# An encoder layer on one core: h made in token order, GpSimd's products moved, and the first expert's bias added last

## The chip, the core and the metric

One core of a Trainium2 chip runs one layer on 256 frames. The metric is the time of one execution in microseconds (us), the median of the runs.

## What is computed

The layer has a stem, a mixer of two head groups, and a mixture of experts; each ends in a LayerNorm with a residual (ALPHA is the fourth root of 2):

```
h = layer_norm(x, ln_in_g, ln_in_b)                       # x: 256 x 1024
gq, gk, gv, gg, glr, rq, rk, rv, rg = split(h @ w_in)     # 3088 columns
o_gla = rms_norm(chunk_attention(gq, gk, gv, decay(glr))) * silu(gg)
o_ret = group_norm(chunk_attention(rotary(rq), rotary(rk), rv, fixed decay)) * silu(rg)
h = layer_norm(ALPHA * h + concat(o_gla, o_ret) @ w_out)
gates = softmax(top4(h @ router_w + router_b))            # 32 experts
for each expert e of a frame:                             # 1024 -> 2048 -> 1024
    y += gate * (clamped_swiglu(h @ w1[e] + b1[e]) @ w2[e] + b2[e])
out = layer_norm(ALPHA * h + y)
```

## The kernel before

**Stages.** The stem normalises x in token order (tile `xt`), turns it by eight TensorE transposes per half of the frames, applies scale and shift per channel from the columns `cols`, and splits the result into a high part `hTh` and a low part `hTl` (`hT`, lines 211 to 248). Every large product of the mixer is made as three products (high x high, low x high, high x low), in `proj_T` (line 255: channels by frames, for gqk, rqk and the two gates) and `values` (line 352: frames by channels, for gv and rv). `split` (line 198) makes the two parts of a piece of weight: ScalarE copies the high part, VectorE (for the first two pieces of gqk GpSimd) subtracts for the low one; three buffers of high parts and two of low ones turn over. `keep_warm` puts transposes of the identity on TensorE, 18, 18 and 14 of them, in the stem.

GpSimd also makes the residual copy `res` of h (lines 333 to 336, from two broadcast loads of 512 KB of scale and shift), four of the decay products and copies in the gated group (lines 381 to 392), the rotation of rq and rk (lines 399 to 404, behind eight ScalarE copies that swap halves), four products in the second gate group (line 537), and the low parts of the biases (`bt`, lines 662 to 672).

**Experts.** The experts go in 16 pairs of up to 64 seats an expert. For a pair, `gather` (line 693) picks the rows by one-hot products into `px` and turns them into `xg`, `hidden` (line 738) puts the bias into four PSUM banks (`set_bias`) and adds the products of w1 in eight k steps, and `outputs` does the same for w2. `in_order` holds TensorE to program order here. The gate softmax is in `finish_routing` (line 674), run from `middle(0)` behind the second k step of pair 0.

**Loads.** All loads go out on SP in order. Weights of the experts, 1 MB a load, go into a ring of 20 buffers (`order`, line 842) that are the mixer's own buffers until it frees them; after the first 21 loads each next one waits until TensorE has used a buffer. The order on each engine comes from a scheduler; `issue_after` puts an instruction behind another of its engine.

Of the kernel before, what the change touches and what calls it, by code (L numbers as in the profile page):

```python
# [12 lines left out]
F32 = mybir.dt.float32  # L13
# [7 lines left out]
P = 128  # L21
# [6 lines left out]
E = 32  # L28
# [5 lines left out]
WARM = (18, 18, 14)  # L34
# [9 lines left out]
def tile_layer(ctx: ExitStack, tc: tile.TileContext, x, positions, rows_d, bc_d, gate_d, w_in, wglr_d,  # L44
# [46 lines left out]
    for t in range(NT):  # L91
        nc.sync.dma_start(xt[:, t, :], x[0, t * P:(t + 1) * P, :])
# [4 lines left out]
    gatew, glrT = gatew[0:32], glrT[0:32]  # L97
    nc.sync.dma_start(rows[:NROW], rows_d)
# [3 lines left out]
    nc.sync.dma_start(posi, positions.to_broadcast([P, S]))  # L102
# [5 lines left out]
    w_gqk = w_cols(0, "w_gqk", (0, 1))  # L108
    nc.sync.dma_start(w_glr, wglr_d.rearrange("p (k n) -> p k n", k=KC))
    nc.sync.dma_start(gatew, gate_d)  # L110
# [19 lines left out]
    G.memset(glrT, 1.0)  # L130
# [23 lines left out]
    cols = const.tile([P, NROW], F32, name="cols")  # L154
    pc = bank("m", "pc")
    pc_done = T.transpose(pc[:, :NROW], rows[:NROW], ident[:NROW, :NROW])
    cols_done = A.activation(cols, pc[:, :NROW], AF.Copy)
    keep_warm(WARM[1], pc_done)
# [15 lines left out]
    def rstd_act(var, name):  # L174
# [5 lines left out]
        newton(y, w, None, vh)  # L180
        return y
# [14 lines left out]
    highs = []  # L196

    def split(src, k, n, name, into=None, eng=V):
# [5 lines left out]
        with tc.issue_after(first_h.ins) if len(highs) == 2 else ExitStack():  # L204
            highs.append(A.activation(hi, src, AF.Copy))
        eng.tensor_sub(lo, src, hi.bitcast(F32))
# [4 lines left out]
    hTh, hTl, hT = (slot(i, nm, dt).rearrange("p (q t k s) -> p q t k s", q=2, t=NT, k=4)  # L211
                    for i, nm, dt in ((11, "hTh", F32R), (12, "hTl", F32R), (14, "hT", F32)))
    pts = {}
    for t in range(NT):
# [4 lines left out]
        with tc.issue_after(cols_done.ins) if t else ExitStack():  # L219
            r = rstd_act(mv[:, 1:2], f"ln0_{t}")  # L220
        V.tensor_scalar(xt[:, t, :], xt[:, t, :], mv[:, 0:1], r, op0=ALU.subtract, op1=ALU.mult)
    preload(TRIG, rstd_exp[-1])
    for t in range(NT):
        for q in range(2):
            pts[t, q] = bank("h", f"phT{t}{q}").rearrange("p (k t) -> p k t", k=4)
            for k in range(4):
                c = 4 * q + k
                last_tr = T.transpose(pts[t, q][:, k, :], xt[:, t, c * P:(c + 1) * P], ident)
    keep_warm(WARM[2], last_tr)
    for q in range(2):  # L230
        for t in range(NT):
            for k in range(4):
                c = 4 * q + k
                gs, bs = cols[:, GIN + c:GIN + c + 1], cols[:, BIN + c:BIN + c + 1]
                if (q, t) == (0, 1):
                    A.activation(hT[:, q, t, k, :], pts[t, q][:, k, :], AF.Identity, bias=bs, scale=gs)
                else:
                    with tc.issue_after((second if t else lead).ins) if q else ExitStack():
                        V.tensor_scalar(hT[:, q, t, k, :], pts[t, q][:, k, :], gs, bs, op0=ALU.mult, op1=ALU.add)
            if (q, t) == (0, 0):  # L240
                lead = V.tensor_copy(hTh[:, q, t], hT[:, q, t])
            else:
                last_h = A.activation(hTh[:, q, t], hT[:, q, t], AF.Copy)
                if q == 0:
                    first_h = last_h
            last_l = (V if t or q else G).tensor_sub(hTl[:, q, t], hT[:, q, t], hTh[:, q, t].bitcast(F32))
            if (q, t) == (0, 1):
                second = last_l
# [6 lines left out]
    def proj_T(w, name, early=False):  # L255
# [12 lines left out]
        return ps, mm  # L268

    (pq, pk_), gqk_mm = proj_T(w_gqk, "gqk", early=True)  # L270
# [3 lines left out]
    s10 = slot(10, "ln_in")  # L274
    bg, bb = cut(s10, (D, D), (None, None))
    for v, i in ((bg, 0), (bb, 1)):
        nc.sync.dma_start(v, bc_d[i:i + 1, :].to_broadcast([P, D]))
# [8 lines left out]
    for j, pr in enumerate(proj_T(w_rqk, "rqk")[0]):  # L286
        A.activation(raw1 if j else raw0, pr, AF.Copy, scale=0.125 if j else 1.0)
# [8 lines left out]
    with tc.issue_after(last_l.ins):  # L296
# [20 lines left out]
    ghi, glo = split(w_glr, KC, 16, "glr")  # L317
    for i, (a, b) in enumerate(((ghi, hTh), (glo, hTh), (ghi, hTl))):
        for k in range(KC):
            T.matmul(pglr[0:16, 0:S].rearrange("p (t s) -> p t s", t=NT), a[:, k, :], chunk(b, k), start=(k == 0 and i == 0), stop=(k == KC - 1 and i == 2))  # L320
    V.tensor_copy(glrT[0:16, :], pglr[0:16, 0:S])
# [9 lines left out]


    res = const.tile([P, NT, D], F32, name="res")
    for t in range(NT):
        G.tensor_mul(res[:, t, :], xt[:, t, :], bg)
        G.tensor_add(res[:, t, :], res[:, t, :], bb)
# [15 lines left out]
    def values(w, v, name):  # L352
        pv = [bank("h", f"p_{name}{t}") for t in range(NT)]
        for k in range(KC):
            hi, lo = split(w[k // 4][:, k % 4:k % 4 + 1, :], 1, 512, f"{name}{k}")
            for t in range(NT):
# [7 lines left out]
    values(w_gv, gv, "gv")  # L364
# [7 lines left out]
    V.tensor_copy(ends, b4[:, :, CH - 1:CH])  # L372
# [702 lines left out]
```

## Time and profile before

| | before |
|---|---|
| median of 3 runs | 1105.64 us |
| lowest and highest run | 1101.23 and 1106.08 us |
| the profiled execution, its own time | 1102.8 us |
| its span, first to last instruction | 1101.0 us |
| matmul busy on TensorE (PE) | 1013.8 us (92%) |
| VectorE (DVE) busy | 284.2 us (26%) |
| ScalarE (ACT) busy | 170.4 us (15%) |
| GpSimd (POOL) busy | 70.8 us (6%) |
| loads on the SP queue | 423.81 MB, 94.5% of the 16 DMA engines' span |

A busy share is an average over the whole span; the mixer fills the first 160 us, the experts the rest. PE's ends are modelled, so a busy PE is not PE at its peak. Idle time is put down to what ended last before it.

### The profile page before, as it was taken

The numbers are of one execution on the slowest core, as the hardware profiler recorded it, in microseconds if no ns is written. First come the engines' busy times: TensorE is split into PE (matmuls) and PEld (weight loads), VectorE is DVE, ScalarE is ACT, GpSimd is POOL, SyncE is SP. The second block draws the span as 40 slices with busy tenths as digits, with TensorE's granted clock in tenths as the row PEclk, the third lists the DMA queues.
The fourth block names the chain that finished last, engine by engine and source line by source line (L and its number), as shares of the span: only waits on it lengthen the run. The fifth ranks groups of instructions, "written<-read, shape, count | busy, mean of one in ns | idle before, by whom it ended". The sixth has DMA issues, their size and how long they took to land. (4 is left out here: it accounts for less than half of the span.)

```text
span 1101.0 us, 12046 instructions
## 1 busy us (share of the span) xinstructions
PE 1013.8 (92%) x4896; PEld 462.2 (42%) x4896; DVE 284.2 (26%) x572; ACT 170.4 (15%) x347; POOL 70.8 (6%) x115
## 2 busy tenths in 40 slices
PE   7889989999999999999999999898989898999974
PEld 7768863333333343243424243333333342434322
DVE  7666951120202030321112020212010120202014
ACT  4465531101010101010101010101001010111010
POOL 5130320000000000000000000000000000000001
PEclk9889999999999999899999999999999999989997
DMA  9835869999999999999999999999999999999993
GB/s 333 327 115 197 332 232 383 420 419 419 420 419 419 420 420 419 420 420 419 420 421 418 419 421 419 418 421 419 418 420 421 419 419 421 419 419 421 419 375 128
DMA packets 70574, 424.65 MB, mean 386 GB/s; under 512 B 7187, under 2 KB 11758, under 8 KB 22382
## 3 DMA queue, kind: packets, MB, share of 16 engines
q1 hardware_dynamic: 70512, 423.81, 94.5%
q8 instruction: 40, 0.66, 0.2%
q14 instruction: 22, 0.18, 0.0%
HBM read 422.74 MB, written 1.05 MB: 385 GB/s over the span
## 5 line engine op out<-in xcount | busy, mean ns | idle before, releaser
L724 PE MATMUL ph<-w,xg 128*64 128x512 f32 x2048 | 471.1, 602 | 31.8 <-DMA w<-in_moe_w_dram 31.6
L724 PEld LDWEIGHTS ph<-w,xg 128*64 128x64 f32 x2048 | 150.4, 138 | 342.9 <-issue 273.8
L724 PE MATMUL py<-w,aT 128*64 128x512 f32 x960 | 217.4, 609 | 0.0
L836 DVE TENSOR_TENSOR acc<-acc,po 128x512 f32<-128x512 f32 (+1 forms) x62 | 41.5, 670 | 392.3 <-PE po L832 392.3
L724 PEld LDWEIGHTS py<-w,aT 128*64 128x64 f32 x960 | 70.9, 140 | 137.0 <-issue 133.7
L766 DVE TENSOR_SCALAR glu<-ph 128x512 f32<-128x512 f32 x32 | 22.0, 687 | 330.6 <-PE ph L724 330.6
L767 ACT ACTIVATE ph<-glu 128x512 f32<-128x512 f32 x32 | 19.3, 602 | 534.9 <-DVE glu L766 534.9
L703 PEld LDWEIGHTS px<-hot,res 128*128 128x128 f32 x512 | 58.4, 192 | 13.0 <-DVE glu L769 11.4
L703 PE MATMUL px<-hot,res 128*128 128x128 f32 x512 | 61.6, 278 | 0.7 <-DVE hot L709 0.7
L832 PE MATMUL po<-y,gT 128*128 128x512 f32 (+1 forms) x132 | 59.8, 594 | 0.5 <-ACT y L965 0.5
L795 ACT ACTIVATE y<-py 128x512 f32<-128x512 f32 x30 | 17.9, 597 | 216.7 <-PE py L724 216.7
L735 POOL CAST bsel<-sel 128x128 fp32r<-128x128 f32 x16 | 4.6, 289 | 633.6 <-PE py L730 623.4
L832 PEld LDWEIGHTS po<-y,gT 128*128 128x128 f32 x132 | 23.6, 189 | 36.0 <-issue 34.9
L730 PE MATMUL py<-bt,bsel 64*128 64x512 f32 x30 | 14.7, 495 | 18.2 <-ACT aT L778 18.2
L716 ACT ACTIVATE xg<-px,cols 128x128 f32<-128x128 f32 x64 | 24.0, 456 | 46.5 <-PE px L703 46.5
L803 POOL TENSOR_TENSOR hog<-hot,gate 128x128 f32<-128x128 f32 x32 | 12.2, 400 | 210.8 <-PE pg L807 202.9
L768 DVE TENSOR_SCALAR ph<-ph 128x512 f32<-128x512 f32 x32 | 22.2, 694 | 2.4 <-PE ph L724 1.3
L718 DVE TENSOR_SCALAR xg<-px,cols 128x128 f32<-128x128 f32 x64 | 21.8, 402 | 2.8 <-PE px L703 2.8
L770 DVE SCALAR_TENSOR_TENSOR glu<-ph,glu 128x512 f32<-128x512 f32 x32 | 21.9, 685 | 0.6
L769 DVE TENSOR_TENSOR glu<-glu,ph 128x512 f32<-128x512 f32 x32 | 21.6, 675 | 0.0
L777 PE MATMUL pa<-ident,glu 128*128 128x128 f32 x128 | 18.3, 284 | 2.0 <-DVE glu L770 2.0
L777 PEld LDWEIGHTS pa<-ident,glu 128*128 128x128 f32 x128 | 16.6, 207 | 3.1 <-DVE glu L770 3.1
(293 smaller groups left out, 711.3 us busy)
## 6 DMA issues: line engine op xcount, KB each, us to landing
w<-in_moe_w_dram SPq DMA_DIRECT2D x376, 1024.0 KB, 19.9
w_out<-in_w_out_dram SPq DMA_DIRECT2D x4, 1024.0 KB, 6.6
w<-in_moe_w_dram SPq DMA_DIRECT2D x8, 512.0 KB, 14.8
w<-in_moe_w_dram SPq DMA_DIRECT2D x16, 256.0 KB, 6.2
w_gqk<-in_w_in_dram SPq DMA_DIRECT2D x2, 1024.0 KB, 10.0
w_rqk<-in_w_in_dram SPq DMA_DIRECT2D x2, 1024.0 KB, 11.6
w_gv<-in_w_in_dram SPq DMA_DIRECT2D x2, 1024.0 KB, 14.6
w_rv<-in_w_in_dram SPq DMA_DIRECT2D x2, 1024.0 KB, 16.2
```

The lines of the kernel that those rows point to most:

```text
L703: in_order(lambda: T.matmul(px[c // 4][:, c % 4, :], res[:, t, c * P:(c + 1) * P], hot[:, t, :], start=(t == 0 and c % 4 == 0), stop=(t == ...
L716: A.activation(xg[:, c, :], px[c // 4][:, c % 4, :], AF.Identity, bias=bs, scale=gs)
L718: V.tensor_scalar(xg[:, c, :], px[c // 4][:, c % 4, :], gs, bs, op0=ALU.mult, op1=ALU.add)
L724: in_order(lambda: T.matmul(ps[i * CAP:(i + 1) * CAP, :], lhs[:, k, i * CAP:(i + 1) * CAP], ws[i], start=False, stop=last, skip_group_chec ...
L766: V.tensor_scalar(glu, pglu, 7.0, None, op0=ALU.min)
L767: sig = A.activation(pglu, glu, AF.Sigmoid, scale=1.702)
L768: V.tensor_scalar(plin, plin, 7.0, -7.0, op0=ALU.min, op1=ALU.max)
L769: V.tensor_mul(glu, glu, pglu)
L770: V.scalar_tensor_tensor(glu, plin, 1.0, glu, op0=ALU.add, op1=ALU.mult)
L777: in_order(lambda: T.transpose(pa[:, k, :], units[:, k // 2, k % 2, :], ident))
L832: in_order(lambda: T.matmul(po[:, 0:n], gT[:, t, :], y[:, at:at + n], start=True, stop=True))
L836: V.tensor_add(acc[:, t, at:at + n], acc[:, t, at:at + n], po[:, 0:n])
```

## The change

**The stem.** The two halves of x go out on two queues. Scale and shift of the stem come as one row (`gb0`), and four one-row products spread them over all frames in PSUM. VectorE centres, scales and shifts in token order, straight into `res`, in halves of the channels (`centred`, `stem`); the transposes then read `res`, and both parts of h come from PSUM. The second half of the channels is made inside the first projection. `cols` is made there too. The warm-up transposes become 10, 8 and 6.

**The mixer.** The halves of rq and rk are swapped by eight DMAs on SP, and the load of W_out's third quarter now waits for the rotation, whose buffer it takes. The decay products go between the splits of rv as `fill`, all on VectorE, the copies on ScalarE; the rotation is all VectorE's. The gate's low rank takes 16 products of 48 and 16 columns instead of 24 of 16. Half of the gated group's scaling by the norm goes to ScalarE, and in the second gate group ScalarE scales and VectorE multiplies.

**The first expert.** The bias splits come behind the gathered rows (`load_biases`, from `middle(0)`), their low parts on VectorE; pair 0 adds its bias last; the gate softmax is issued behind `xg`.

```
-WARM = (18, 18, 14)
+WARM = (10, 8, 6)
...
-        nc.sync.dma_start(xt[:, t, :], x[0, t * P:(t + 1) * P, :])
+        (nc.scalar if t else nc.sync).dma_start(xt[:, t, :], x[0, t * P:(t + 1) * P, :])
+    gb0 = slot(10, "ln_in").rearrange("p (a n) -> p a n", a=2)
+    nc.scalar.dma_start(gb0[0:1], bc_d.rearrange("(o a) n -> o a n", o=1))
...
+            spread_ = T.matmul(spreads[a, q], ones[0:1, :], gb0[0:1, a, q * 512:(q + 1) * 512], start=True, stop=True)
...
+    def centred(t, q):
...
+            return V.scalar_tensor_tensor(res[:, t, qs], xt[:, t, qs], mvs[t][:, 0:1], spreads[0, q], op0=ALU.subtract, op1=ALU.mult)
...
+    def stem(q):
...
+                lasts["n"] = V.scalar_tensor_tensor(res[:, t, qs], res[:, t, qs], rs[t], spreads[1, q], op0=ALU.mult, op1=ALU.add)
...
+                    lasts["t"] = T.transpose(pt[:, k, :], res[:, t, c * P:(c + 1) * P], ident)
+            lasts["h"] = A.activation(hTh[:, q, t], pt, AF.Copy)
+            lasts["l"] = V.tensor_sub(hTl[:, q, t], pt, hTh[:, q, t].bitcast(F32))
...
+                if early and not kh:
+                    lasts["p"] = mm
+                    stem(1) if j == 0 else columns()
...
+        for q in range(4):
+            nc.sync.dma_start(swaps[j][32 * q:32 * q + 32], raw[32 * (q ^ 1):32 * (q ^ 1) + 32])
...
+    for k in range(KC):
+        for n, b in ((48, hTh), (16, hTl)):
+            T.matmul(pglr[0:n, 0:S].rearrange("p (t s) -> p t s", t=NT), ghl[:, k, 0:n], chunk(b, k),
...
-    for t in range(NT):
-        G.tensor_mul(res[:, t, :], xt[:, t, :], bg)
-        G.tensor_add(res[:, t, :], res[:, t, :], bb)
...
-    G.tensor_mul(qn, gqT, enb)
-    V.tensor_mul(kn, gkT, enb)
-    G.tensor_mul(ke, gkT, eb)
...
+    rv_mm, rv_done = values(w_rv, rv, "rv", (decays, own_keys, own_queries, end_keys, lambda: V.tensor_mul(ke, gkT, eb),
+                                             lambda: V.tensor_mul(qn, gqT, enb), cross))
...
-        G.tensor_mul(swp, swp, sin[:, None, :].to_broadcast([P, 2, S]))
-        G.tensor_add(rot, rot, swp)
+    for swp, rot in zip(swaps, (rotq, rotk)):
+        with tc.issue_after(lows[-1].ins):
+            V.tensor_mul(swp, swp, sin[:, None, :].to_broadcast([P, 2, S]))
+        V.tensor_add(rot, rot, swp)
...
-                    G.tensor_mul(pr_, pr_, sl[:, h, :])
+                    A.activation(pr_, pt[:, h, :], AF.Identity, bias=cols[:, RB + c:RB + c + 1], scale=cols[:, RG + c:RG + c + 1])
+                    V.tensor_mul(pr_, pr_, sl[:, h, :])
...
+            with tc.issue_after(lasts["xa"].ins):
+                A.activation(bt[:, a, :], bs, AF.Copy)
+            for r0 in (32, 96):
+                V.tensor_sub(bt[r0:r0 + 32, a, :], bs[r0:r0 + 32], bt[r0:r0 + 32, a, :].bitcast(F32))
...
+            with tc.issue_after(lasts["xv"].ins):
+                V.tensor_scalar(ex, lx[:, t, 0:E], top[:, t, 4:5], None, op0=ALU.subtract)
...
+        if bias_last:
+            for j, b in enumerate(blocks):
+                set_bias(ps[j], bsel, b, last=True)
```

How it moves instructions is seen at three places. GpSimd between the first splits and the routing, before (`gqk_l` are the low parts of w_gqk, `res` the residual copy, `gfac` and `gcross` the decay products):

```order
L206 TENSOR_TENSOR gqk_l<-w_gqk_74,gqk_h 128x512 x2
L246 TENSOR_TENSOR hTl<-hT,hTh 128x512
L335 TENSOR_TENSOR res<-xt,ln_in 128x1024 x2
L336 TENSOR_TENSOR res<-res,ln_in 128x1024 x2
L330 MEMSET gqk 64x4x64
L403 TENSOR_TENSOR logs<-logs,gcross 128x512
L404 TENSOR_TENSOR misc<-misc,logs 128x512
L403 TENSOR_TENSOR logs<-logs,gcross 128x512
L383 TENSOR_TENSOR gfac<-gqk,decays 128x512
L381 TENSOR_TENSOR gfac<-gqk,decays 128x512
L392 COPY gcross<-gfac 128x2x64
```

and now:

```order
L214 TENSOR_TENSOR gqk_l<-w_gqk_74,gqk_h 128x512 x2
L315 CAST gscore<-rscore 128x256
L356 MEMSET gqk 64x4x64
L539 TENSOR_TENSOR misc_945<-misc_945,cols 128x256
L540 TENSOR_TENSOR misc_945<-misc_945,cols 128x256
```

The large operations of GpSimd between its first splits and the router's weights are gone from its queue.

VectorE in the second value product, as it stands now (`rv_l` are the low parts of w_rv, `decays` the exponentials):

```order
L214 TENSOR_TENSOR rv_l<-w_rv_361,rv_h 128x512 x2
L415 TENSOR_TENSOR gfac<-gqk,decays 128x512
L419 TENSOR_TENSOR gfac<-gqk,decays 128x512
L214 TENSOR_TENSOR rv_l<-w_rv_361,rv_h 128x512
L423 TENSOR_TENSOR gcross<-gqk,decays 128x512
L214 TENSOR_TENSOR rv_l<-w_rv_363,rv_h 128x512
L432 TENSOR_TENSOR gfac<-gqk,decays 128x512
L214 TENSOR_TENSOR rv_l<-w_rv_363,rv_h 128x512
L433 TENSOR_TENSOR gfac<-gqk,decays 128x512
L214 TENSOR_TENSOR rv_l<-w_rv_363,rv_h 128x512
```

Each decay product stands behind one split, and the five products of 512 columns are all here.

TensorE at the first expert, before (`px` are the gathered rows, `ph` the four banks of the first expert's product):

```order
L703 MATMUL px_1613<-hot_1610,res 128x128 x4
L730 MATMUL ph_1645<-bt,bsel_1643 128x512
L730 MATMUL ph_1646<-bt,bsel_1643 128x512
L730 MATMUL ph_1647<-bt,bsel_1643 128x512
L730 MATMUL ph_1648<-bt,bsel_1643 128x512
L724 MATMUL ph_1645<-w_00_0_1653,xg_1611 64x512
```

and now:

```order
L746 MATMUL px_1550<-hot_1547,res 128x128 x4
L767 MATMUL ph_1582<-w_00_0_1586,xg_1548 64x512
L767 MATMUL ph_1582<-w_01_0_1588,xg_1548 64x512
L767 MATMUL ph_1583<-w_00_0_1586,xg_1548 64x512
L767 MATMUL ph_1583<-w_01_0_1588,xg_1548 64x512
```

The four bias products no longer stand between the gathered rows and the first product of w1.

## Rows read from the trace of the kernel before

**Rows 1.** Busy time by stretch: stretch, us, busy per engine, PEclk, DMA share, GB/s.

```profile
166.04:1065.00 898.96, 846.77 (x3858) 327.00 (x3854) 154.70 (x289) 83.17 (x174) 16.70 (x46) 0.98 1.01 418
...
161.00:167.00 6.00, 6.00 (x22) 1.82 (x20) 0.20 (x1) 0.63 (x1) 2.48 (x2) 0.72 0.05 16
...
32.00:38.15 6.15, 6.13 (x28) 6.14 (x29) 3.54 (x8) 2.72 (x6) 0.00 (x0) 0.50 1.05 381
```

**Rows 2.** Timeline of SP at the first expert: start us, us, instruction.

```profile
157.55 1.80 SPq L669 DMA_DIRECT2D bs<-in_bias_dram  x4
166.04 3.76 SPq L914 DMA_DIRECT2D w<-in_moe_w_dram  x3
```

**Rows 3.** Waits of SP from 150 to 215: us in total, times, longest.

```profile
SPq L914 <- PE ph L724: 9.2, 2, 6.7
```

**Rows 4.** Timeline of PE, first projections; in brackets the idle time before and its releaser.

```profile
15.01 0.71 PE L265 MATMUL p_gqk<-hTh,gqk_h 128*128 128x256 f32 x4 [0.34 <-ACT hTh L243]
...
25.45 0.63 PE L265 MATMUL p_gqk<-hTh,gqk_h 128*128 128x256 f32 x4
32.02 1.22 PE L265 MATMUL p_gqk<-hTh,gqk_l 128*128 128x256 f32 x4 [5.94 <-DVE gqk_l L206]
...
39.61 0.63 PE L265 MATMUL p_rqk<-hTh,rqk_l 128*128 128x256 f32 x4
40.09 0.63 PE L265 MATMUL p_rqk<-hTl,rqk_h 128*128 128x256 f32 x4
```

**Rows 5.** Timeline of POOL: residual copy of h, and a decay product.

```profile
21.24 5.34 POOL L335 TENSOR_TENSOR res<-xt,ln_in 128x1024 f32<-128x1024 f32 x2 [5.01 <-DMA ln_in<-in_bc_dram]
26.54 4.87 POOL L336 TENSOR_TENSOR res<-res,ln_in 128x1024 f32<-128x1024 f32 x2
...
69.31 1.71 POOL L381 TENSOR_TENSOR gfac<-gqk,decays 128x512 f32<-128x512 f32 x1
```

**Rows 6.** The tile w_gqk, VectorE's splits: shortest/median/longest in ns, first and last start.

```profile
L206 DVE TENSOR_TENSOR gqk_l<-w_gqk,gqk_h x6: 679/682/2823, 18.6 to 32.7; 128x512 fp32r<-128x512 f32 x6
```

**Rows 7.** Timeline of PE, second value product.

```profile
64.66 0.39 PE L358 MATMUL p_rv<-rv_h,hTh 128*128 128x512 f32 x1
64.89 0.39 PE L358 MATMUL p_rv<-rv_h,hTl 128*128 128x512 f32 x1
...
73.61 1.22 PE L358 MATMUL p_rv<-rv_l,hTh 128*128 128x512 f32 x2 [3.81 <-DVE rv_l L206]
...
84.28 0.33 PE L419 MATMUL lo<-gfac 64*64 64x64 f32 x4
```

**Rows 8.** Timeline of PE, output projection.

```profile
137.89 0.73 PE L548 MATMUL pm<-wo_l,oTh 128*128 128x512 f32 x2 [0.96 <-DVE wo_l L206]
```

**Rows 9.** Timeline of PE, bias and first expert's product.

```profile
158.91 0.50 PE L730 MATMUL ph<-bt,bsel 64*128 64x512 f32 x2 [1.29 <-POOL bt L672]
160.25 0.49 PE L730 MATMUL ph<-bt,bsel 64*128 64x512 f32 x1 [0.84 <-POOL bt L672]
160.67 8.78 PE L724 MATMUL ph<-w,xg 128*64 128x512 f32 x32
```

**Rows 10.** Timeline of VectorE there, four pieces of gathered rows.

```profile
157.47 1.36 DVE L718 TENSOR_SCALAR xg<-px,cols 128x128 f32<-128x128 f32 x4
```

**Rows 11.** Timeline of VectorE in the stem, statistics of the second half.

```profile
5.98 1.29 DVE L217 BATCH_NORM_STATS2 ln_st<-xt 128x6 f32<-128x512 f32 x2
```

**Rows 12.** Lines 821 and 884: one-row spread, and VectorE's pass that reads it (ns).

```profile
L821 PE MATMUL h<-gb,ones x8: 587/718/1214, 441.4 to 447.3; 1*128 1x512 f32 x8
...
L884 DVE SCALAR_TENSOR_TENSOR h<-res,h x4: 676/678/686, 442.6 to 446.8; 128x512 f32<-128x512 f32 x4
```

**Rows 13.** Timeline of PE in the stem: warm-up and transposes.

```profile
7.60 3.79 PE L151 MATMUL warm<-ident 128*128 128x128 f32 x18
11.23 1.91 PE L228 MATMUL phT<-ident,xt 128*128 128x128 f32 x16
```

**Rows 14.** Timeline of PE, gate rank.

```profile
49.50 1.08 PE L320 MATMUL pglr<-hTh,glr_l 128*16 128x256 f32 x8
```

More of the change, by code (lines that the diff above doesn't have):

```diff
@@ L153, in tile_layer @@
     keep_warm(WARM[0])
[L154 to L158, printed above, removed]
+    spreads = {}
+    for q in range(2):
+        for a in range(2):
+            spreads[a, q] = bank("h", f"gb0{a}{q}")
+            spread_ = T.matmul(spreads[a, q], ones[0:1, :], gb0[0:1, a, q * 512:(q + 1) * 512], start=True, stop=True)
+    keep_warm(WARM[1], spread_)
     def small(name, n, tag, dt=F32):
@@ L179, in rstd_act @@
         rstd_exp.append(A.activation(y, y, AF.Exp, scale=-0.5))
-        newton(y, w, None, vh)
+        with tc.issue_after(after().ins) if after else ExitStack():
+            newton(y, w, None, vh)
         return y
@@ L226, in tile_layer @@
             for k in range(4):
                 c = 4 * q + k
[L228 to L248, printed above, removed]
@@ new lines, in stem, with columns @@
+                with tc.issue_after(lasts["p"].ins) if q else ExitStack():
+                    lasts["t"] = T.transpose(pt[:, k, :], res[:, t, c * P:(c + 1) * P], ident)
+            lasts["h"] = A.activation(hTh[:, q, t], pt, AF.Copy)
+            lasts["l"] = V.tensor_sub(hTl[:, q, t], pt, hTh[:, q, t].bitcast(F32))
+    stem(0)
+    for t in range(NT):
+        centred(t, 1)
+    first_h = lasts["h"]
+    keep_warm(WARM[2], lasts["t"])
+    cols = const.tile([P, NROW], F32, name="cols")
+    def columns():
+        pc = bank("m", "pc")
+        with tc.issue_after(lasts["p"].ins):
+            T.transpose(pc[:, :NROW], rows[:NROW], ident[:NROW, :NROW])
+        A.activation(cols, pc[:, :NROW], AF.Copy)
@@ L316, in tile_layer @@
     pglr = bank("m", "pglr")
[L317 to L321, printed above, removed]
+    ghl = hl.tile([P, 512], F32R, name="glr_hl", tag="wh", bufs=WH)[:, 0:KC * 48].rearrange("p (k n) -> p k n", k=KC)
+    A.activation(ghl, ident[:, 0:48][:, None, :].to_broadcast([P, KC, 48]), AF.Copy, scale=0.0)
+    A.activation(ghl[:, :, 0:16], w_glr, AF.Copy)
+    V.tensor_sub(ghl[:, :, 32:48], w_glr, ghl[:, :, 0:16].bitcast(F32))
+    for k in range(KC):
+        for n, b in ((48, hTh), (16, hTl)):
+            T.matmul(pglr[0:n, 0:S].rearrange("p (t s) -> p t s", t=NT), ghl[:, k, 0:n], chunk(b, k),
+                     start=(k == 0 and n == 48), stop=(k == KC - 1), skip_group_check=True)
+    V.tensor_copy(glrT[0:16], pglr[0:16, 0:S])
+    A.activation(glrT[32:48], pglr[32:48, 0:S], AF.Copy)
     lg = [math.log1p(-2.0 ** (-5.0 - h)) for h in range(4)]
@@ L392, in tile_layer @@
[L392 to L404 removed]
+    last_exp = [None]
@@ L736, in selector, with hidden @@
         return bsel
-    def hidden(xg, sel2, load, name, mid=None, early=None):
+    def hidden(xg, sel2, load, name, mid=None, early=None, bias_last=False):
         bsel = selector(sel2, name)
@@ L745, in hidden @@
         ps = [bank("h", f"ph{name}{b}") for b in blocks]
-        for j, b in enumerate(blocks):
-            set_bias(ps[j], bsel, b)
+        if not bias_last:
+            for j, b in enumerate(blocks):
+                set_bias(ps[j], bsel, b)
         for k in range(KC):
```

152 lines of the change are left out of this document (80 added, 72 removed).

## The prediction

> **What bounds the kernel now.** I read the page's slices first, then the busy times by stretch, then the issue queue of the loads, and last TensorE's order of time through the mixer. From 166 us on, the DMA engines are full (share 1.01, 418 GB/s) for 899 us, up to the tail of some 36 us [rows 1]. All of this is expert weights. So the end is the moment at which this stream starts, plus a length that the change does not touch, and any microsecond taken from the work before 166 us should come off the end, if the stream has nothing to catch up. It has not: just before, from 161 to 167 us, the DMA share is 0.05 [rows 1]. The ring of weight buffers is full then, and the next load goes out at 166.04, after a bias load at 157.55 [rows 2]; what it waited for is the first expert's product, up to 6.7 us at a time [rows 3]. That product starts at 160.67 [rows 9].
>
> So the question is when the first expert's product can start, and the mixer's stalls answer it. TensorE starts the first projection at 15.01, stands for 5.94 us before 32.02 until VectorE has split a piece of w_gqk [rows 4], and then runs at half clock (0.50, 1.2 GHz) until 38.15 [rows 1]. VectorE was late because its 0.68 us subtraction took up to 2.82 [rows 6] while GpSimd made the residual copy of h, 10.2 us in two rows [rows 5]. The same happens at 69 to 73.6: GpSimd multiplies decays [rows 5], TensorE waits 3.81 us for VectorE, then goes on slowly [rows 7]. Then comes a wait of 0.96 in the output projection [rows 8], and the bias rows: 1.29 and more on GpSimd's splits, although the gathered rows were coming from 157.47 on [rows 9, 10].
>
> **The change, part by part.**
>
> *Stem.* Before, 15.01 [rows 4]. Now the second half of x goes on another queue, and VectorE can hardly begin its statistics earlier than 5.98 [rows 11]; with 1.29 of them and three small operations I come to 7.8. Then two centring and two scaling passes, each like the one pass in the trace that reads SBUF and a spread row in PSUM, 0.68 [rows 12], so 2.7, and four one-column operations, together about 0.5: 11.0. A transpose is 0.12, sixteen in 1.91 [rows 13], so four of them, a copy taken as another 0.68, and the hops between the engines bring the first product to 12.6. Against it, the spread products stand ahead on TensorE: four of two passes each, 0.59 at best and 1.21 at worst for a pass, which overlap [rows 12], behind a row that lands at 6.5 or so, and eight warm products at 0.21 [rows 13]; that ends at 11 to 13 and may hold the transposes up by a microsecond or two. I take 13.3: a gain of 1.7. Ends: none of it (the four passes held up by GpSimd's two weight splits, 2.1 more, as the subtraction of [rows 6] was: -0.4), and 2.7.
> [...]
>
> *First projections.* Before, from 15.01 to 40.09 [rows 4] there are 30 groups of four products. At the pace of 39.61 to 40.09, 0.47 to 0.48 a group [rows 4], they take 14.1. Eight transposes of the second half of h now stand between them, 1.0 [rows 13], and one of the columns, 0.1: 15.2 against 25.08, a gain of 9.9, if VectorE keeps up without GpSimd's residual work beside it. Its list up to the end of gqk holds 14 passes of 0.68 and eight small ones of at most half that, 12.2, against TensorE's 12.4: tight, but the splits stand early in it. Ends: 5.0 (VectorE's list laid behind TensorE's waits, and the clock down once more) and 10.5.
>
> *Gate rank.* Three times eight products become sixteen; eight took 1.08, the pace 0.115 each [rows 14]: 0.9 less, ends 0.5 and 0.9.
>
> *Values.* Before, the second value product runs from 64.66 to 84.28 [rows 7], 19.62. It holds 48 products at 0.23 [rows 7] and a gate group of 0.47: 11.75. All of the decay products now stand on VectorE between the splits, copies on ScalarE, nothing on GpSimd. VectorE's list there is 14 passes of 0.68 and four narrow ones, some 11 to 12: again about TensorE's own time, with two buffers of slack. The rotation's swap goes from ScalarE to eight DMAs, off its path; they ride behind loads, but are read only after the last value split. I take 7.9, ends 4.0 (VectorE bound, TensorE standing for a microsecond or two, and its clock down behind it) and 8.2.
>
> *Output gates.* GpSimd's four products go to VectorE and its scaling to ScalarE; two engines, no row shows the pair, but the 0.96 of [rows 8] is the only wait there. I take 1.0 with 0 as the lower end: TensorE is busy otherwise from 84.28 on.
>
> *Bias.* The first product no longer waits for the bias rows, which are added last for pair 0. It can go when the first of the four pieces of 157.47 [rows 10] is there, at 158.0, not 160.67 [rows 9]: 2.7. Ends 2.0 and 3.5 (the gate softmax is off VectorE ahead of the pieces, too). The gate softmax then stands before the transposes of the gate behind two k steps, 8.8 us of products [rows 9]; VectorE's and GpSimd's work for it is nearer 6 and lies under that. The third bias load stays ahead of the next weight load on SP and now waits for VectorE's two first bias splits, some 3.5 us behind the first product with issue; the weight load behind it waited 5.4 for the product anyway [rows 2, 9]. Costed at nothing; if the splits come later, the stream does, one for one.
>
> *One-row loads.* A megabyte of spread scale and shift leaves the load queue, one load of W_out moves behind the rotation, tens of microseconds before its split is due; both at nothing.
>
> Sum: 1.7 + 9.9 + 0.9 + 7.9 + 1.0 + 2.7 = 24.1. The profiled execution took 1102.8, 2.8 under the median of its runs (1105.64). 1102.8 - 24.1 = **1078.7**. With all lower ends the gain is 11.1 (1091.7), with all upper ones 26.8 (1076.0). Runs lie from 1.6 below to 3.3 above the profiled one.
>
> **Rivals.**
> *VectorE becomes the bound* in gqk and the values, where both lists are within a microsecond of TensorE's. For it: these counts, and that a wait of a few microseconds was followed by half clock both times [rows 1, 7]. Against: the splits are spread out. A gain of 12 to 20, so some 1087.
> *The bias part does nothing,* since the third bias load holds SP ahead of the weights. For it: its place in the queue. Against: 5.4 us of cover [rows 2, 9]. The gain of 2.7 goes and up to two more: 1083.
> *The weights are not there.* The swaps and the late load of W_out hold SP, and the ring is short when the first expert starts. Each missing load of 1 MB is 2.5 us at 418 GB/s; four to ten of them give back 10 to 24: 1090 to 1103. Against: the idle 6 us of [rows 1], and slack in the queue all through the mixer.
> *Slower: the clock.* Warm products fall from 50 to 24, and TensorE stands idle until the row for the spread has landed. In the trace the first 36 transposes went at 0.21 to 0.23 and only those from 11.23 on at 0.12 [rows 13]. If the clock stays low from the first projection on, each microsecond of it costs half: 1078.7 plus half the stretch. It is slower than before only if it stays low for over 48 us, through the values; 63 us would give 1110. Against: behind a stand of 5.94 it came back after 6.15 [rows 1, 4].
> The Trainium skill (TensorE: Matmul & The Clock Gate, What's actually happening) says that "the default state is throttled, and activity releases the throttle". By that page the thinner warm-up is this rival's condition, while the products that follow without a stop release it, so the page leaves it a small chance.
>
> **How the numbers follow.** 0.5%, 5.5 us, is about what a measurement of this kernel can tell from no change. Forecast (1076 to 1083) 0.60; VectorE bound 0.22; bias part nothing 0.06; weights not there 0.06, a third of it under 1097; clock 0.03; and 0.03 for better than 1076. Faster: 0.60 + 0.22 + 0.06 + 0.03 + 0.02 = 0.93; same 0.04; slower 0.03. The range takes in all bounds and the scatter of the runs below: 1073 to 1092.
>
> **What would show it.** In the profile after: the first projection near 13.3, no wait over a microsecond in gqk and the values, a clock of 1.00 through the mixer, VectorE's subtractions at 0.68 throughout, the first expert's product near 137 (160.67 - 24.1 is 136.6), full DMA from some 142 on, and the same tail. The prediction is wrong if full DMA begins early and the end does not follow, or if a wait of TensorE for VectorE stands where GpSimd's work was.

## The result, and the profile after

The changed kernel takes 1084.45 us (median of four runs, 1083.38 to 1084.75), the kernel before 1104.12 (four runs, 1101.23 to 1106.08): a ratio of 0.9829, 95% interval 0.9805 to 0.9853. The forecast was 1078.7, with a range of 1073 to 1092. The profiled execution took 1084.73 instead of 1102.8: 18.1 us of the 24.1 that the sum had. So the time lies within the range, but above the band of 1076 to 1083 that had the largest chance.

Busy time by stretch of the kernel after, to be read beside [rows 1] (stretch, us, busy per engine, PEclk, DMA share, GB/s):

```profile
6.00:13.20 7.20, 7.15 (x9) 2.52 (x9) 7.13 (x18) 3.19 (x7) 1.72 (x2) 1.00 1.02 346
32.00:38.15 6.15, 6.15 (x54) 6.15 (x54) 3.10 (x7) 6.00 (x12) 0.31 (x1) 1.00 1.05 381
...
147.13:1047.00 899.87, 846.99 (x3854) 327.80 (x3850) 157.90 (x296) 83.75 (x175) 16.97 (x47) 0.98 1.01 418
1047.00:1082.90 35.90, 20.42 (x115) 9.59 (x115) 13.86 (x30) 4.61 (x9) 3.04 (x2) 0.83 0.50 166
```

The full stream is as long as before (899.87 and 898.96 us, 418 GB/s both), it only starts sooner, and the stretch from 32.00 to 38.15 that ran at 0.50 now holds 54 products instead of 28, at 1.00. The loss is in the first line: in these 7.2 us TensorE did nine things.

The stem of the kernel after, timeline of PE, answering to the first lines of [rows 4] and to [rows 13]:

```profile
6.05 7.19 PE L164 MATMUL gb<-ln_in,ones 1*128 1x512 f32 x8 [1.82 <-DMA ln_in<-in_bc_dram]
13.17 1.97 PE L156 MATMUL warm<-ident 128*128 128x128 f32 x8
14.93 1.91 PE L250 MATMUL phT<-ident,res 128*128 128x128 f32 x8
16.64 1.49 PE L156 MATMUL warm<-ident 128*128 128x128 f32 x6
17.77 1.20 PE L282 MATMUL p_gqk<-hTh,gqk_h 128*128 128x256 f32 x4
...
21.84 1.04 PE L250 MATMUL phT<-ident,res 128*128 128x128 f32 x8
```

Eight passes of the spread take 7.19 us, 0.9 each, and eight transposes 1.91, where eight of the same shape take 1.04 a little later (at 21.84). So, by these lengths, TensorE runs at 1.2 GHz through the whole stem. The column PEclk shows 1.00 there; in the stem the lengths of equal products have to be read, not that column. VectorE had the first half of the channels of h at 12.15, and the transposes began at 14.93. Timeline of VectorE, the statistics of the first half of the frames, and the two passes that end at 12.15:

```profile
5.88 1.28 DVE L233 BATCH_NORM_STATS2 ln_st<-xt 128x6 f32<-128x512 f32 x2 [5.88 <-DMA xt<-in_x_dram]
...
10.74 1.41 DVE L244 SCALAR_TENSOR_TENSOR res<-res,ln_y,gb 128x512 f32<-128x512 f32 x2
```

Later places of the same timeline, which answer to [rows 4], [rows 7] and [rows 9] (first projections' last group and the gate rank behind it; start of the second value product and what follows it; first expert's product):

```profile
41.95 0.63 PE L282 MATMUL p_rqk<-hTl,rqk_h 128*128 128x256 f32 x4
42.42 0.27 PE L344 MATMUL pglr<-hTh,glr_hl 128*48 128x256 f32 x1
...
57.02 0.48 PE L382 MATMUL p_rv<-rv_h,hTh 128*128 128x512 f32 x1
...
69.33 0.33 PE L455 MATMUL lo<-gfac 64*64 64x64 f32 x4
...
141.60 7.09 PE L767 MATMUL ph<-w,xg 128*64 128x512 f32 x32
```

Between 17.77 and 135 us TensorE has no wait long enough for the timeline to name one; before, the longest were 5.94, 3.81, 0.98 and 0.96. VectorE's splits, by tile, show why; the first answers to [rows 6]:

```profile
L214 DVE TENSOR_TENSOR gqk_l<-w_gqk,gqk_h x6: 681/692/693, 19.8 to 28.3; 128x512 fp32r<-128x512 f32 x6
...
L214 DVE TENSOR_TENSOR rv_l<-w_rv,rv_h x8: 682/688/693, 55.5 to 66.2; 128x512 fp32r<-128x512 f32 x8
```

None takes longer than 0.693 us; the longest was 2.82 before. And the issue queue of the loads at the first expert, beside [rows 2]:

```profile
145.31 1.73 SPq L710 DMA_DIRECT2D bs<-in_bias_dram  x4
147.13 1.91 SPq L962 DMA_DIRECT2D w<-in_moe_w_dram  x3
```

The third bias load went out 3.71 us behind the first product and the weight load behind it at 5.53; before, the weight load was 5.37 behind (166.04 and 160.67). That is 0.16 later, next to nothing, as costed.

### The profile page after: what moved, and what is told of

It reads as the page before. It is cut to its first block, busy times and chain, and to the rows that moved or that the text cites. A ratio compares the mean times of both kernels' runs of the same rounds, so it can differ in the third digit from the quotient of the medians.

```text
span 1082.9 us, 11976 instructions
## 1 busy us (share of the span) xinstructions
PE 1009.8 (93%) x4870; PEld 457.6 (42%) x4870; DVE 273.1 (25%) x574; ACT 168.9 (16%) x350; POOL 36.1 (3%) x90
## 5 line engine op out<-in xcount | busy, mean ns | idle before, releaser
L883 DVE TENSOR_TENSOR acc<-acc,po 128x512 f32<-128x512 f32 (+1 forms) x62 | 41.6, 671 | 391.5 <-PE po L879 391.4
L879 PEld LDWEIGHTS po<-y,gT 128*128 128x128 f32 x132 | 23.6, 189 | 36.0 <-issue 34.9
L759 ACT ACTIVATE xg<-px,cols 128x128 f32<-128x128 f32 x64 | 24.1, 458 | 44.6 <-PE px L746 44.6
```

The source lines that it names most:

```text
L759: lasts["xa"] = A.activation(xg[:, c, :], px[c // 4][:, c % 4, :], AF.Identity, bias=bs, scale=gs)
L879: in_order(lambda: T.matmul(po[:, 0:n], gT[:, t, :], y[:, at:at + n], start=True, stop=True))
L883: V.tensor_add(acc[:, t, at:at + n], acc[:, t, at:at + n], po[:, 0:n])
```

## The experiments

Four questions: what holds the stem (seven runs), what the products on GpSimd cost (four runs), what the bias order alone is worth (one run). And in all of them: does the end follow the first expert's product? Each run has one profile. Beside these runs the kernel before took 1102.75 to 1103.71 (medians), against 1104.12 beside the changed kernel, and four runs of one kernel lie 0.5 to 4.3 us apart; so times a microsecond or two apart tell little, and the readings rest on the profiles.

### The stem

**No warm-up between spread and transposes.**

```diff
-WARM = (10, 8, 6)
+WARM = (10, 0, 6)
```

> The eight warm-up products between the spread and the transposes are taken out (WARM 10, 0, 6). Theory: TensorE's own list sets the first projection. In the changed kernel VectorE has the first half of h at 12.15 us and the transposes begin at 14.93, behind a spread of 7.19 and eight warm products of 1.76; so without them the transposes begin at 13.2, the first projection near 16.1 instead of 17.77, and the end comes 1.7 earlier, 1082.7. Rival, the clock: those eight are what makes the clock rise before 18.8; without them the first projection starts 1.7 earlier but runs at the pace of half clock (0.23 a product) for about as much longer, and the end stays at 1084.4.

Timeline of PE in the stem, and the first expert's product:

```profile
13.19 1.97 PE L250 MATMUL phT<-ident,res 128*128 128x128 f32 x8
...
16.09 0.92 PE L282 MATMUL p_gqk<-hTh,gqk_h 128*128 128x256 f32 x4
...
139.20 7.09 PE L767 MATMUL ph<-w,xg 128*64 128x512 f32 x32
```

1082.03 us (1081.89 to 1085.6). The first projection starts at 16.09, 1.68 sooner. By the last transposes (19.68 for 21.84) the lead has grown to 2.16, because the products were at full pace from the second group on (0.63 for four), and the first expert's product comes 2.40 sooner. So TensorE's own list set the stem; the rival, that the eight products were needed for the clock, falls.

**Twenty warm-up products first**, run twice, the second time unchanged.

```diff
-WARM = (10, 8, 6)
+WARM = (20, 8, 6)
```

> The first warm-up is 20 products instead of 10 (WARM 20, 8, 6), so that TensorE does not stand idle from 4.23 to 6.05 ahead of the spread; they end near 6.4. Theory one, the spread is slow because nothing ahead of it has raised the clock: its passes fall from 1.06 to near 0.59, the spread ends near 11 instead of 13.24, the eight warm products and transposes go at 0.12, and the first projection starts 3 to 4 us earlier, 1080.5 to 1081.5. Theory two, products of one row do not count for the clock, whatever stands ahead of them: the spread stays at 7 us, starts 0.4 later, and the time is 1084.8.

> The kernel with 20 first warm-up products once more, unchanged (WARM 20, 8, 6), for a second look. If the 20 products decide: the spread takes 3.9 again and the first projection starts near 14.2. If the clock in the stem differs from run to run: 7.2 and 17.9 to 18.2. Either way the last weights are in some 900 us behind the first expert's product, and what is left is the tail, 41 to 45 us long.

Timeline of PE in the first of the two, and below it the stretch behind its spread:

```profile
6.29 3.85 PE L164 MATMUL gb<-ln_in,ones 1*128 1x512 f32 x8
10.07 1.97 PE L156 MATMUL warm<-ident 128*128 128x128 f32 x8
11.83 1.67 PE L250 MATMUL phT<-ident,res 128*128 128x128 f32 x8
...
14.19 0.74 PE L282 MATMUL p_gqk<-hTh,gqk_h 128*128 128x256 f32 x4
```

```profile
10.07:12.50 2.43, 2.43 (x13) 2.43 (x13) 2.43 (x7) 1.88 (x3) 0.98 (x1) 0.50 0.96 272
```

The spread runs in 3.85 us (3.90 in the second run), then the clock falls to 0.50 behind it, although TensorE did not stand still: the eight warm products take 1.97 again. The first projection starts at 14.19 and 14.42, the first expert's product at 137.05 and 137.31, some 4.4 sooner than in the changed kernel. The time is 1083.57 (1081.35 to 1085.61) and 1082.74 (1081.76 to 1085.49): a gain of 0.9 and 1.7, less than that. The last section of this part says where the rest went.

**Both edits together**, `WARM = (20, 0, 6)`.

> Both edits together (WARM 20, 0, 6). If TensorE's list sets the stem and a longer first warm-up raises the clock: the transposes wait for VectorE at 12.2 and go at 0.12, the first projection starts near 14.5, 3.3 earlier than in the changed kernel, 1081. If the warm-up does not raise the clock: 1.3 earlier, 1083.1. If the second warm-up is what raises it: no gain, 1084.4.

1082.65 us. The program is the same as the one above up to the spread's end, and starts it at the same 6.29, but here the spread took 7.19:

```profile
6.29 7.19 PE L164 MATMUL gb<-ln_in,ones 1*128 1x512 f32 x8
```

So twenty products raise the clock in time in some runs and not in others; the first projection starts at 16.31, and the first expert's product at 140.01.

**The last spread product behind the transposes**, instead of the warm-up there.

```diff
-WARM = (10, 8, 6)
+WARM = (20, 0, 0)
...
-    for q in range(2):
-        for a in range(2):
...
+    for a, q in ((0, 0), (1, 0), (0, 1)):
+        spread_row(a, q)
...
     stem(0)
+    spread_row(1, 1, lasts["t"])
```

> The changed kernel with the last of the four spread products (the second half's shift) moved behind the first transposes in place of the six warm-up products there, no warm-up between spread and transposes, 20 warm-up products first (WARM 20, 0, 0). If the stem runs at half clock: three spread products end near 11.7, the transposes wait for VectorE at 12.2, and the first projection starts at 15.0 to 16.0 (17.77 in the changed kernel): 1081.5 to 1083. If the clock has risen by the spread, as in one of two runs that begin with the same 20 products: 14.0 to 14.5, and 1080.5 to 1081.5. Rival: fewer warm products leave the clock low into the first projections, and the start gained is lost behind it: 1084 or more.

1087.26 us (1086.66 to 1087.59). The three spread products ended at 9.1, TensorE stood 2.61 us for VectorE, and from there on it was at 0.50 until 19.2:

```profile
11.73 1.97 PE L253 MATMUL phT<-ident,res 128*128 128x128 f32 x8 [2.61 <-DVE res L247]
...
15.62 1.22 PE L286 MATMUL p_gqk<-hTh,gqk_h 128*128 128x256 f32 x4
```

```profile
15.00:17.00 2.00, 2.00 (x7) 1.38 (x7) 1.32 (x3) 0.00 (x0) 0.00 (x0) 0.50 1.05 388
```

The time is the one that the rival with fewer warm products gave, but its reason is only part of it. The first projection started 2.15 sooner than in the changed kernel, and the second value product still ended 1.2 sooner (68.11 and 69.33), so the slow first projections took back 0.9. The rest went where the clock was down once more between 130 and 141.7 (0.85 as a mean), so that the first expert came at 141.72, no sooner than 141.60. The 2.8 us by which the time is longer are nearly all in the tail (44.2 for 41.6).

**A spread of 128 rows.** The first with `WARM = (25, 8, 6)`, the second with the changed kernel's own warm-up.

```diff
+    nc.vector.memset(gb0, 0.0)
     nc.scalar.dma_start(gb0[0:1], bc_d...
...
-            spread_ = T.matmul(spreads[a, q], ones[0:1, :], gb0[0:1, a, ...
+            spread_ = T.matmul(spreads[a, q], ident[:, 0:1].to_broadcast([P, P]), gb0[:, a, ...
```

> The spread's products read 128 rows instead of one: the tile of the scale and shift row is set to zero by VectorE ahead of its load, and a column of the identity, repeated, stands in for the ones, so that the result is the same; 25 warm-up products first, up to the row's later landing (WARM 25, 8, 6). Theory, a product of one row does not hold TensorE's clock (behind both spreads that ran fast the records show 0.50): with 128 rows the clock stays up once it has risen, no record of 0.50 from 6 to 20 us, spread near 3.9, transposes at 0.12 from VectorE's 12.5 on, the first projection at 14.2 to 15.2, the first expert's product at 137.5 to 139. Rival, the clock falls whatever the rows are, since it depends on other things (the idle time, the run): a record of 0.50, or a spread of 7.2, and the first projection at 16 to 18.

> The same spread of 128 rows, with the changed kernel's own warm-up (WARM 10, 8, 6). Theory: the spread's own products now raise the clock: its later passes go at 0.5 instead of 0.9, it ends 1 to 3 us sooner behind the row's landing than 7.19, the warm products and transposes behind it go at 0.12, and the first projection starts at 14.5 to 16 instead of 17.77. Rival: rows do not matter; the spread takes 7.19 as in five runs of five that began with 10 warm products, and the first projection starts near 18.5, later by the row's later landing.

The first of the two, timeline of PE, and its clock from the spread to the first projection:

```profile
8.02 3.67 PE L165 MATMUL gb<-ln_in,ident 128*128 128x512 f32 x8 [0.81 <-DMA ln_in<-in_bc_dram]
...
12.40 1.04 PE L251 MATMUL phT<-ident,res 128*128 128x128 f32 x8
...
14.17 0.74 PE L283 MATMUL p_gqk<-hTh,gqk_h 128*128 128x256 f32 x4
```

```profile
8.02:14.17 6.15, 6.07 (x30) 3.87 (x30) 5.91 (x15) 4.32 (x10) 2.72 (x3) 1.00 1.05 352
```

No 0.50 behind this spread; the transposes take 1.04, the first projection starts at 14.17, the first expert's product at 137.07. 1080.36 us (1079.47 to 1081.93), the best of the study, 0.9797 of the kernel before (0.9768 to 0.9827); of its four runs the slowest is below the fastest of the changed kernel, though they were taken beside other runs of the kernel before (1102.75 and 1104.12). Set against those, the two ratios have intervals that overlap (0.9768 to 0.9827, and 0.9805 to 0.9853), so a gain over the changed kernel is likely and not settled by the times. In the second, the spread begins slowly and becomes fast on the way:

```profile
7.66 5.38 PE L165 MATMUL gb<-ln_in,ident 128*128 128x512 f32 x8 [3.44 <-DMA ln_in<-in_bc_dram]
...
15.53 0.74 PE L283 MATMUL p_gqk<-hTh,gqk_h 128*128 128x256 f32 x4
```

With one row and the same 10 warm products it was 7.19 in six profiles of six, from first pass to last; with 128 rows there is this one profile. The first expert's product came at 138.44, 3.2 sooner than in the changed kernel; the time is 1084.13 all the same (1082.9 to 1085.41).

### GpSimd beside VectorE

**GpSimd's residual work put back beside the first projections.**

```diff
+    extra = slot(14, "extra").rearrange("p (t n) -> p t n", t=NT)
+    for t in range(NT):
+        G.tensor_mul(extra[:, t, :], xt[:, t, :], res[:, t, :])
+        G.tensor_add(extra[:, t, :], extra[:, t, :], res[:, t, :])
```

> Added to the changed kernel: four GpSimd operations of 128x1024 with two inputs in SBUF, as the residual copy of the kernel before had them, on x and h into a tile that nothing reads, from about 19.5 us on. Theory (the price of the first-projection term): GpSimd slows VectorE's subtractions from 0.68 to between 2 and 2.8, TensorE stands for 4 to 6 us and falls to half clock behind it; the first expert's product comes 6 to 9.5 later than 141.60 and the time is 1090 to 1094. Rival: the wait of the kernel before came from VectorE's own list (scale, shift and split of h), and GpSimd's work lies beside the others' for nothing: VectorE's subtractions stay at 0.68 and the time is 1084.4.

1089.13 us (1088.04 to 1090.3). Timeline of VectorE, then of GpSimd:

```profile
19.79 5.08 DVE L214 TENSOR_TENSOR gqk_l<-w_gqk,gqk_h 128x512 fp32r<-128x512 f32 x2
24.79 0.68 DVE L252 TENSOR_TENSOR hTl<-phT,hTh 128x512 fp32r<-128x512 f32 x1
25.39 2.27 DVE L214 TENSOR_TENSOR gqk_l<-w_gqk,gqk_h 128x512 fp32r<-128x512 f32 x1
```

```profile
19.11 5.21 POOL L293 TENSOR_TENSOR extra<-xt,res 128x1024 f32<-128x1024 f32 x2 [4.61 <-DVE res L244]
24.27 5.62 POOL L294 TENSOR_TENSOR extra<-extra,res 128x1024 f32<-128x1024 f32 x2
```

The subtractions of two SBUF tiles took 2.27 to 2.88, while the one that reads PSUM and SBUF took 0.68 beside the same GpSimd work. But TensorE stood only 0.69, 0.91 and 0.75 us, did not lose its clock, and the first expert's product came 2.94 later (144.54). The theory is right on the mechanism and too large in size. VectorE beside the residual copy in the kernel before shows what differs:

```profile
21.57 2.77 DVE L206 TENSOR_TENSOR gqk_l<-w_gqk,gqk_h 128x512 fp32r<-128x512 f32 x1
24.26 2.47 DVE L300 TENSOR_SCALAR gscore<-gscore 128x256 f32<-128x256 f32 x1
26.77 2.44 DVE L305 SCALAR_TENSOR_TENSOR gscore<-gscore 128x256 f32<-128x256 f32 x1
29.14 2.82 DVE L206 TENSOR_TENSOR gqk_l<-w_gqk,gqk_h 128x512 fp32r<-128x512 f32 x1
```

The splits took about as long there as here. But between the last two, two small operations on the rotary angles (`gscore`) stood in the list, and they took 2.47 and 2.44, where the changed kernel has 0.29 and 0.42 for them. By these numbers that is 4.2 us, an estimate of their part in the 5.94 that TensorE waited. In the run here the same operations came behind GpSimd's work, from 30.37 on, and two of the operations between the splits read PSUM. So, in these rows, each VectorE operation that was held took about as long as one of GpSimd's beside it (2.4 to 2.8), the short ones too: their number counts there, not their length.

**Decays back on GpSimd, ahead of the splits; and the order alone, all on VectorE.** The diff is that of the first; the second issues the same parts in one go ahead of `values`, all products on VectorE and the copies on ScalarE.

```diff
-    rv_mm, rv_done = values(w_rv, rv, "rv", (decays, own_keys, own_queries, end_keys, ...
+    decays()
+    V.tensor_mul(qe, gqT, eb)
+    G.tensor_mul(qn, gqT, enb)
...
+    rv_mm, rv_done = values(w_rv, rv, "rv")
```

> In the changed kernel the decay part is put back as it was: two products and four copies on GpSimd, all of it issued ahead of the second value product's splits instead of between them. Theory (the values term): VectorE's subtractions of w_rv wait for GpSimd again, TensorE stands 3 to 5 us in the second value product and falls to half clock behind it; the product takes 16 to 20 us instead of 12.3, the first expert's product comes 4 to 7.5 later than 141.60, the time is 1088 to 1092. Rival: with the residual copy gone the queue has slack enough, the product stays at 12.3 to 13 and the time at 1084.4 to 1085.

> Order alone: every decay product stays on VectorE and the copies on ScalarE, but all are issued ahead of the second value product's splits, so that four products stand in a row ahead of the third split. Theory one, the engine decides (GpSimd's work beside VectorE's was the cost): the second value product stays within 1.5 us of 12.3 and the time at 1084 to 1086. Theory two, the place between the splits decides: TensorE waits 2 to 4 us for the third split, falls to half clock, and the time is 1088 to 1091, like the kernel with the products back on GpSimd.

With GpSimd: 1086.45 us, the second value product 14.57 (56.06 to 70.63) against 12.31 in the changed kernel, two waits of 1.46 and 0.27, no fall of the clock:

```profile
63.36 0.73 PE L382 MATMUL p_rv<-rv_l,hTh 128*128 128x512 f32 x2 [1.46 <-DVE rv_l L214]
```

With the order alone: 1084.36 us, 12.97 (56.34 to 69.31), one wait of 0.26. So of the 2.3 us the engine makes 1.6 and the place between the splits 0.7. Together they are a third of what the values part had gained. The product began 0.7 to 1.0 sooner in these two runs, since the first projections were that much quicker, so the first expert's product shows less of it: 142.59 and 141.27, for 141.60.

**The whole values part as before**: the above, and the rotation on GpSimd with its swap as ScalarE copies.

```diff
-        for q in range(4):
-            nc.sync.dma_start(swaps[j][32 * q:32 * q + 32], raw[32 * (q ^ 1):32 * (q ^ 1) + 32])
...
+            A.activation(swp[32 * q:32 * q + 32], raw[32 * (q ^ 1):32 * (q ^ 1) + 32], AF.Copy)
...
+        G.tensor_mul(swp, swp, sin[:, None, :].to_broadcast([P, 2, S]))
+        G.tensor_add(rot, rot, swp)
```

> The changed kernel with the whole values part as it was before: decay products and copies on GpSimd ahead of the splits (as in the run with the decays back on GpSimd, which lost 2.3 us in the second value product), and besides the rotation on GpSimd and its swap as eight ScalarE copies instead of DMAs. Theory: the rotation's products and the swap copies carry the rest of the 7.3 us between the kernels; GpSimd's chain runs from the first value product into the second, TensorE stands 3 to 5 us and falls to half clock, the second value product takes 17 to 20 us instead of 12.3, the first expert's product comes 4.5 to 7.5 later than 141.60, and the time is 1088.5 to 1092. Rival: the decays were all that the values part gives, the rest came from the residual copy's lag or the state of the clock: the second value product takes 14 to 15.5 us, and the time stays at 1086 to 1087.

1088.55 us (1088.4 to 1088.85). Timeline of GpSimd, of VectorE beside it, and TensorE's wait:

```profile
61.11 1.75 POOL L431 TENSOR_TENSOR gfac<-gqk,decays 128x512 f32<-128x512 f32 x1
62.81 1.74 POOL L449 TENSOR_TENSOR misc<-misc,logs 128x512 f32<-128x512 f32 x1
64.52 1.70 POOL L433 TENSOR_TENSOR gfac<-gqk,decays 128x512 f32<-128x512 f32 x1
```

```profile
61.62 1.78 DVE L432 TENSOR_TENSOR gfac<-gqk,decays 128x512 f32<-128x512 f32 x1
63.33 1.78 DVE L430 TENSOR_TENSOR gfac<-gqk,decays 128x512 f32<-128x512 f32 x1
65.03 1.75 DVE L434 TENSOR_TENSOR gcross<-gqk,decays 128x512 f32<-128x512 f32 x1
```

```profile
68.54 1.18 PE L379 MATMUL p_rv<-rv_l,hTh 128*128 128x512 f32 x2 [3.90 <-DVE rv_l L214]
```

VectorE's products, 0.68 alone, end at 63.40, 65.11 and 66.78: 0.54 to 0.56 behind each GpSimd operation, as if the two took turns. The second value product takes 19.22 (56.20 to 75.42), having begun 0.8 sooner than in the changed kernel; the first expert comes at 147.33, 5.73 later. That is nearly the 19.62 of the kernel before, made again in the changed kernel. The chain is the rotation's products on GpSimd, which wait for the swap copies of ScalarE (they start at 56.13 and 59.83, each behind one), and the decays behind them.

### The bias order alone

The kernel before, where pair 0 adds its bias last; nothing else.

```diff
-        for j, b in enumerate(blocks):
-            set_bias(ps[j], bsel, b)
+        if not bias_last:
...
+        if bias_last:
+            for j, b in enumerate(blocks):
+                set_bias(ps[j], bsel, b, last=True)
```

> The kernel before with one part of the change: pair 0 adds its bias last; the bias splits stay where they were, on GpSimd. Theory (the bias term): the first expert's product starts when the first gathered rows are there, at 157.1 to 158.0 instead of 160.67, and the end comes 2.7 to 3.6 earlier, 1099 to 1100 beside 1102.8. Rival: the gain needs the gate softmax behind the gathered rows too, or the third bias load gives it back; less than 1.5 is gained, 1101.3 or more.

1099.51 us (ten runs), 0.9969 of the kernel before (0.9952 to 0.9986). The first expert's product starts at 157.81, and no longer at 0.80 of the clock (7.09 us for what took 8.78):

```profile
157.81 7.09 PE L724 MATMUL ph<-w,xg 128*64 128x512 f32 x32 [1.18 <-DVE xg L718]
```

From the second gathering products (155.16 before, 154.60 here, 139.65 in the changed kernel) it is 5.51, 3.21 and 1.95 us to that start. So adding the bias last is worth 2.3. The other 1.3 was not run by itself; the trace of this run puts it to the gate softmax, which VectorE finished at 157.4, just ahead of the gathered rows. Two of its operations took 1.29 and 1.08 there beside GpSimd's bias splits, where the same two, for the other half of the frames, took 0.17 and 0.24 earlier. So both moves count, the softmax behind the rows and the splits off GpSimd.

### Does the end follow?

In the fourteen profiles the first expert's product starts between 137.05 and 160.67; from there to the start of the last product that waits for weights it is 899.0 to 900.5 us in all of them (1059.81 - 160.67 = 899.14 before, 1041.31 - 141.60 = 899.71 after). One for one, over 23.6 us. What is left behind that product, the tail, is 40.3 to 44.9 us, and it makes up for part of what was gained: 41.2 before, 41.6 after, 44.9 and 43.3 in the two runs with 20 first products, 44.2 with the late spread, 41.5 and 44.8 with 128 rows. The run with 128 rows and 10 products shows where, in its last large product (the changed kernel has 7.09 for the same):

```profile
1047.39 9.44 PE L768 MATMUL py_last<-w,aT 128*64 128x512 f32 x32
...
1047.39:1056.83 9.44, 9.44 (x34) 2.81 (x33) 0.00 (x0) 0.00 (x0) 0.00 (x0) 0.75 0.95 305
```

TensorE waits for weights three times ahead of it, 1.3 to 1.4 us each, and its clock comes back sooner or later. Why later in these profiles was not settled, nor that it belongs to the kernels: each tail is that of one execution, and runs of one kernel differ as much (1081.89 to 1085.6 without the second warm-up).

## Why the prediction was right, and where it was off

The terms, from the two profiled executions (the starts stand in [rows 4], [rows 7], [rows 14] and in the lines above; the gate rank's first product stood at 48.56 before, the first value product's at 51.33 and 44.24, the first gathering products at 152.06 and 136.55):

| term | forecast | measured |
|---|---|---|
| stem: 15.01 to 17.77 | 1.7 (-0.4 to 2.7) | -2.8 |
| first projections: 33.55 to 24.65 | 9.9 | 8.9 |
| gate rank: 2.77 to 1.82 | 0.9 | 0.95 |
| first value product: 13.33 to 12.78 | 0 | 0.55 |
| values: 19.62 to 12.31 | 7.9 | 7.3 |
| output gates, up to the gathering: 67.78 to 67.22 | 1.0 | 0.6 |
| bias: 8.61 to 5.05 | 2.7 (2.0 to 3.5) | 3.6 |
| sum, the first expert's product | 24.1 | 19.1 |
| stream and tail | 0 | -1.0 |

**The frame held.** The end follows the first expert's product one for one, the last bias load hides behind it, no weights were missing, VectorE did not become the bound. By the time alone one could not tell: 1084.45 stands between the band and the 1087 of the rival in which VectorE is the bound, and only the trace, without a wait of TensorE for VectorE, rules that rival out. That the sum missed by no more is in part luck, since the bias gave 0.9 more than its term and the first value product 0.55 that had none.

**The stem is the step that failed.** The text took the first projection at 13.3 and no later than 15.4. VectorE was 1.1 late (12.15 for 11.0): on two queues the halves of x landed near together (5.0 and 4.8 us behind their issue), and the statistics of the first began at 5.88 instead of 4.43, so that those of both halves stood behind that moment, where the text had put one. The rest is TensorE at 1.2 GHz: I took a transpose at 0.12 and the spread's end with the warm products at 11 to 13, while all of it went at the slow pace and ended at 14.93; and the first product reads both halves of the frames, so eight transposes and two copies stand ahead of it, not four and one. With the clock up (the run with 128 rows and 25 products first) the first projection starts at 14.17, the first expert at 137.07 and the time is 1080.36, where the text had 13.3, 136.6 and 1078.7. So about 3.6 us of the 4.5 that the stem was off are the clock, by that one profile, and some 0.9 the late VectorE and the transposes that the text did not count. The rival about the clock named this cause and its condition, fewer warm products and an idle TensorE, but placed it behind the first projection, where there was little of it: the first two groups took 1.71 for 0.94, and from 19.5 us on every product ran at full pace up to the first expert.

The Trainium skill (TensorE: Matmul & The Clock Gate, What's actually happening) has activity release the throttle. The trace agrees only in part: the clock had not risen after 7.19 us of uninterrupted one-row products in the changed kernel, and with 128-row products in their place it rose within 5.38, in the one profile of that run.

**The first projections and the values** came out within a microsecond, for reasons that were only partly the ones given, and in that part by luck. Of the microsecond that the first projections fell short, 0.8 is the slow clock in their first two groups. Of the 8.9 gained, GpSimd's residual work alone makes 2.9. A large part of the rest lay, by the trace of before, in the two angle operations that stood between the splits and were held as well, which the text did not see; no run tried them alone, nor the half clock behind the wait. Of the 7.3, the decay products that the text named make 2.3; the rotation and its swap, ahead of them in the same chain, make it 6.9 together. The text's own pace for this product gives 11.5 (48 products at 0.23 and 0.47), not its 11.75; it took 12.31.

The Trainium skill (SBUF — State Buffer, Who interferes with whom) says that a VectorE instruction with two SBUF inputs contends with a GpSimd instruction that reads SBUF, and that one with at most one SBUF input does not, outside the modes in which it uses two ports; copies, casts and `tensor_scalar` can be in such a mode. The trace agrees: 2.27 to 2.88 for subtractions of two SBUF tiles, 0.68 for the one with an input in PSUM beside the same work, and before, 2.47 for a `TENSOR_SCALAR` with a single input that takes 0.29 alone.

The stem's passes, with one input in PSUM, kept 0.70 beside GpSimd's split, as costed.

**The bias part** was right and slightly too small (3.6, its upper end was 3.5): it left out of its middle value the gate softmax, to which the trace puts 1.3.

## What to carry to other kernels

Where a later stage is bound by a stream, find the first instruction that releases it and add up what stands ahead of it; here every microsecond there came off the end. Before a VectorE operation gets a price, look at what GpSimd does beside it and whether its inputs are in SBUF, and count the operations that stand there, the short ones too. And where a change alters what TensorE does in its first 20 us, do not carry its pace over from the kernel before: sixteen transposes took 1.91 there, eight took as long after.

## What was not expected of the hardware

- A stretch of one-row products was followed by the half clock in all three profiles in which TensorE had been fast through it (3.85, 3.90 and, for six passes, 2.85 us), twice without any idle time between; one stretch of 3.67 us of 128-row products was not.
- Behind the same 20 warm-up products the one-row spread ran fast in three profiles and at half the pace (7.19) in one, whose program was the same up to there.
- VectorE's 0.68 us products beside GpSimd's 1.7 us ones went as if one at a time with them, each ending some 0.55 us behind the GpSimd operation; an operation of 0.29 us took 2.47 beside GpSimd's of 2.4 to 2.8.
